# A decoder trunk on one core: a tile's square and copy after its low part, and column sums and spreads at other places among the matmuls

## The chip, the cores and the metric

The kernel runs on one core of a Trainium2 chip. The metric is the device time of the program in microseconds (us). Before the change it is 1248.27 us, the median of three runs (1246.43 to 1250.76). The engines are TensorE (PE: matmuls; its weight loads are listed as PEld), VectorE (DVE), ScalarE (ACT), GpSimd (POOL) and SyncE (SP, which issues DMAs). Each works through its own list of instructions in order and waits at the head of that list when something that it needs isn't ready.

## The reference

Two layers over 512 tokens of 1024 channels, in float32. Layer 0 mixes with a gated short convolution and a forgetting attention, layer 1 with a convolution module; each is followed by a SwiGLU feed-forward part. Around every part stands a normalisation before and one after:

```python
def rms_norm(x, g):
    xf = x.astype(jnp.float32)
    y = xf * lax.rsqrt(jnp.mean(xf * xf, axis=-1, keepdims=True) + RMS_EPS)
    return (y * g.astype(jnp.float32)).astype(x.dtype)

u = rms_norm(h, norm_mix_pre[layer])
h = h + rms_norm(m, norm_mix_post[layer])          # m = mixer(u)
f = swiglu_ffn(rms_norm(h, norm_ffn_pre[layer]), w_ffn_in[layer], w_ffn_out[layer])
h = h + rms_norm(f, norm_ffn_post[layer])
```

Between two parts, then, stand the closing norm of one, the residual sum, and the opening norm of the next. The kernel calls this stretch `cross`; this text calls it a handover.

## The kernel before

Channels lie on the 128 partitions, eight tiles `h[k]` of 128 channels, and the 512 tokens along the free side, in two halves of 256 columns. A matmul keeps float32 precision by splitting both operands into a high and a low part (`wh`, `wl`, `xh`, `xl`) and summing three products: high by high, high by low, low by high (`mm3`, lines 197 to 199). Weights arrive in chunks of 512 KB (`ensure`): an SP DMA fills `wr`, ACT rounds it to `wh` (line 175), and DVE (line 177) or POOL (line 180) takes the rest as `wl`. PE's order is the order in which the code is written.

There are three handovers, called H1 to H3 here: after the mixer of layer 0, after the feed-forward part of layer 0, and after the mixer of layer 1. In them ACT, DVE and POOL keep the written order too (`manual_schedule`, line 842). A handover runs so:

- `tail(0)` and `tail(1)` are the last matmuls of the old part, for the first and the second half of the columns. An output `m` that is finished is squared and copied out by ACT (`evict`).
- The squares are summed over the eight `m` in `acc` (line 240: POOL, the last one DVE). Two matmuls with a column of ones give the column sums (line 257, called column sums below). DVE takes a reciprocal root of them in eleven small Newton steps (lines 299 to 309), and two matmuls with the identity spread the result over all partitions (line 317, called a spread).
- `tiles(hf, n)` then makes the new activations of one half, tile by tile. For tile `k`: DVE multiplies the output by the spread (line 707, into `t`), does the low part of the tile before (`low(k - 1)`, line 702, `xl`), and adds the residual (line 712) into `hp`, which stands in one of two PSUM banks by turns; ACT rounds `hp` to the high part `xh` (line 714), squares it for the next norm (line 713's call, seen as line 247), and copies it to `h[k]` (line 717). After the eighth tile, `xl` comes first and copy and square after it (lines 718 to 721). Newton steps of another norm are put between these DVE instructions by `beside()`.
- `quads` multiplies the first four weight chunks of the next part with one half of the columns: eight steps `k` with eight matmuls each on `xh[k]` (lines 794 and 795), then eight steps of four matmuls on `xl[k]` (line 797). It runs for half 0, then for half 1. `pairs` goes on with both halves.
- `weave(units, inserts)` sets the order: after unit `n` of the matmuls stand the instructions whose number is `n`.

So PE stands still at a column sum until the squares are summed, at a spread until the Newton steps are done, and at a step of `quads` until its `xh[k]` is there. `scale_pre` (line 725) puts the spread of the opening norm into `R`, by which every result of `quads` is multiplied when it is taken out (`ready`, `evict`).

Of the kernel before, what the change touches and what calls it, by code (L numbers as in the profile page):

```python
# [10 lines left out]
AF = mybir.ActivationFunctionType  # L11
# [6 lines left out]
NK = D // P  # L18
# [14 lines left out]
MIXF0 = 0  # L33
MIXF1 = 3
MIXF2 = 0
FIRST_TILE = 14
STATS1 = 1
TILES1 = 5
PRE0 = 8
SCALE0 = 2  # L40
PRE1 = 10
SCALE1 = 4
END0 = 5
END1 = 18
# [44 lines left out]
def trunk(tc, x, vec, bands, w_xa, w_in, w_v, w_f, w_out, w_fi, w_fo, w_p1, w_p2, out):  # L89
# [6 lines left out]
    act = nc.scalar.activation  # L96
# [5 lines left out]
    with tc.tile_pool(name="sb", bufs=1) as sb, tc.tile_pool(  # L102
# [4 lines left out]
        def alloc(tag, shape=(P, T), dt=F32, bufs=1):  # L107
            uid[0] += 1
            return sb.tile(list(shape), dt, name=f"{tag}_{uid[0]}", tag=tag, bufs=bufs)
# [46 lines left out]
        def ensure(n, pieces=1):  # L156

            while len(split) < min(n, len(chunks)):
                name, ap, spare = chunks[len(split)]
                count[name] = count.get(name, -1) + 1  # L160
                raw = alloc("wr", (P, D), F32, 2)
                if spare is None:
                    h = alloc("wh", (P, D), FR, 5)
                    l = alloc("wl", (P, D), FR, 5)
                else:
                    if spare == 0:
                        spares[0] = alloc("pth", (P, 2560), FR), alloc("ptl", (P, 2560), FR)
                    h, l = (t[:, spare * D : (spare + 1) * D] for t in spares[0])
                a = ap.shape[1]
                r3 = raw.rearrange("p (a b) -> p a b", a=a)  # L170
                for i in range(pieces):
                    cs = slice(i * D // pieces, (i + 1) * D // pieces)
                    ps = slice(i * a // pieces, (i + 1) * a // pieces)
                    nc.sync.dma_start(r3[:, ps], ap[:, ps])
                    act(h[:, cs], raw[:, cs], AF.Copy)  # L175
                    if (name, count[name]) not in pool_split:
                        tt(out=l[:, cs], in0=raw[:, cs], in1=h[:, cs], op=ALU.subtract)  # L177
                        continue
                    for c in range(i * D // pieces, (i + 1) * D // pieces, HT):
                        nc.gpsimd.tensor_tensor(out=l[:, c : c + HT], in0=raw[:, c : c + HT], in1=h[:, c : c + HT],  # L180
                                                op=ALU.subtract)
                split.append((name, h, l))
# [28 lines left out]
        def col(i, n=1):  # L211
            return vecs[:, i : i + n]
# [47 lines left out]
        def weave(units, inserts=()):  # L260

            todo = list(inserts)
            n = 0
            while todo and todo[0][0] <= 0:
                todo.pop(0)[1]()
            for _ in units:
                n += 1
                while todo and todo[0][0] <= n:
                    todo.pop(0)[1]()
            for _, f in todo:  # L270
                f()
# [40 lines left out]
        def spread(*cols, tag="s", ps=None):  # L312

            if ps is None:
                ps = psum(tag)
            for j, c in enumerate(cols):
                mm(ps[:, j * P : (j + 1) * P], c.to_broadcast([P, P]), ident, start=True, stop=True)
            return ps

        def each(t, n):  # L320
            return [t[:, j : j + 1] for j in range(n)]
# [324 lines left out]
        class Boundary:  # L646
# [19 lines left out]
            def evict(self, m, ps, c0, cn, part=None):  # L666
                cs = slice(c0, c0 + cn)
                extra = {} if self.bias is None else {"bias": col(self.bias + m)}
                src = ps
                with tc.high_priority():  # L670
                    if part is not None:
                        tt(out=self.s[m][:, cs], in0=ps, in1=part[:, cs], op=ALU.add)
                        src = self.s[m][:, cs]
                        extra = {}
                    for c in range(c0, c0 + cn, HT):
                        self.sums.square(c // HT, src[:, c - c0 : c - c0 + HT], m == NK - 1,
                                         room=self.bank(0)[:, HT:] if m == NK - 1 else None, **extra)
                    if part is None:
                        act(self.s[m][:, cs], ps, AF.Identity if extra else AF.Copy, **extra)  # L679
# [12 lines left out]
            def tiles(self, hf, beside):  # L692

                cs = slice(hf * HT, (hf + 1) * HT)
                if hf == 0:
                    self.pre = Sums()
                rp = spread(*each(self.cols[hf], 2), ps=self.bank(1)[:, :HT])
                t = self.bank(1)[:, HT:]

                def low(k):  # L700
                    hp, g = self.hp
                    stt(out=self.x[1][k][:, cs], in0=hp, scalar=g, in1=self.x[0][k][:, cs],  # L702
                        op0=ALU.mult, op1=ALU.subtract)
                    beside()

                for k in range(NK):
                    stt(out=t, in0=self.s[k][:, cs], scalar=col(self.gpost + k), in1=rp, op0=ALU.mult, op1=ALU.mult)
                    beside()
                    if k:
                        low(k - 1)  # L710
                    hp, g = self.hp = self.bank(2 + k % 2)[:, :HT], col(self.gpre + k)
                    tt(out=hp, in0=hin[k][:, cs], in1=t, op=ALU.add)  # L712
                    beside()
                    act(self.x[0][k][:, cs], hp, AF.Copy, scale=g)  # L714
                    if k < NK - 1:
                        self.pre.square(hf, hp, False)
                        act(hin[k][:, cs], hp, AF.Copy)
                    yield
                low(k)
                act(hin[k][:, cs], hp, AF.Copy)  # L720
                self.pre.square(hf, hp, True, room=self.bank(2 + k % 2)[:, HT:])
                yield
# [92 lines left out]
        def cross(bd, tail, name, evict):  # L815


            held, side = {}, [iter(())]

            def beside():  # L820
                next(side[0], None)

            def begin(gen):
                side[0] = gen

            def rest():
                for _ in side[0]:
                    pass

            def ready(hf):  # L830
                bd.scale_pre(hf)
                for p in range(2):
                    evict(p, held[hf][p][:, 0], held[hf][p][:, 1], bd.R, hf * HT, HT)

            def tiles(hf, n):
                if hf not in gens:
                    gens[hf] = bd.tiles(hf, beside)
                for _ in range(n):
                    next(gens[hf], None)

            gens = {}
            with tc.manual_schedule(engines={mybir.EngineType.Activation, mybir.EngineType.DVE, mybir.EngineType.Pool}):
                weave(tail(0))
                base = cursor[0]
                weave(tail(1), [(1, lambda: ensure(base + 3)), (4, lambda: bd.post0(0)), (10, lambda: ensure(base + 4))]
                      + [(FIRST_TILE + 4 * k, lambda: tiles(0, 1)) for k in range(5)])
                w4 = [take(name, 0) for _ in range(4)]
                weave(quads(w4, bd.x, 0, lambda pb, c0, cn: held.update({0: pb})),
                      [(0, lambda: tiles(0, 1)), (STATS1, lambda: begin(bd.stats_post(1))),
                       (STATS1, lambda: (tiles(0, 3), rest())), (TILES1, lambda: (tiles(1, 2), ensure(base + 5))),  # L850
                       (PRE0, lambda: begin(bd.stats_pre(0))), (PRE0, lambda: (tiles(1, 4), ensure(base + 6)))])
                weave(quads(w4, bd.x, 1, lambda pb, c0, cn: held.update({1: pb})),
                      [(0, lambda: (tiles(1, 3), rest())), (SCALE0, lambda: ready(0)),
                       (PRE1, lambda: (begin(bd.stats_pre(1)), rest()))])
                late = [(SCALE1, lambda: ready(1))]
                weave(pairs(name, bd, 2, 3, evict), late)
# [46 lines left out]
        hin = [alloc(f"h{k}") for k in range(NK)]  # L903
        for k in range(NK):
            nc.gpsimd.dma_start(hin[k], x[:, k])
        bd = Boundary(V_MIX_POST, V_FFN_PRE)
# [8 lines left out]
        bd, tail = ffn(bd, g, V_FFN_POST, V_MIX_PRE + 8)  # L915
# [271 lines left out]
        bd = Boundary(V_MIX_POST + 8, V_FFN_PRE + 8, V_PW2)  # L1187
# [12 lines left out]
        bd, tail = ffn(bd, g, V_FFN_POST + 8, None)  # L1200
# [78 lines left out]
```

## Time and profile before

| | |
|---|---|
| median of the runs | 1248.27 us |
| the profiled execution, its own time | 1246.69 us |
| its span | 1244.9 us |
| granted TensorE clock, mean | 0.978 of full speed |
| busy: PE | 1181.4 us, 95% of the span |
| busy: DVE | 670.0 us, 54% |
| busy: ACT | 515.8 us, 41% |
| busy: POOL | 290.3 us, 23% |

PE is busy nearly all the time, and its work is fixed, so what can be had is its idle time and the time in which its clock is at the lower of its two levels (1.2 instead of 2.4 GHz). In the page's 40 slices of 31 us PE shows an 8 or a 7 where the handovers lie (from 218, 622 and 840 us), and the granted clock an 8 in these slices or the one after. The trace is then read around these places.

### The profile page before, as it was taken

How to read it: one execution, taken by the hardware profiler on the slowest of the kernel's cores; microseconds unless marked ns; L12 is line 12 of the kernel's file. 1: busy time of each engine (PE TensorE's matmuls, PEld its weight loads, DVE VectorE, ACT ScalarE, POOL GpSimd, SP SyncE). 2: the span in 40 equal slices, each digit the busy share in tenths (PEclk: the TensorE clock that was granted, in tenths of full speed). 3: DMA queues.
4: the chain of work that ended last, by engine and by line, in shares of the span. 5: the costliest groups of instructions: out<-in, count | busy, mean ns of one | idle time of the engine just before them, and what ended most of it. 6: DMA issues, size and time to landing. Idle time of an engine off the chain costs nothing.

```text
span 1244.9 us, 16224 instructions
## 1 busy us (share of the span) xinstructions
PE 1181.4 (95%) x6134; PEld 1003.2 (81%) x6134; DVE 670.0 (54%) x1240; ACT 515.8 (41%) x958; POOL 290.3 (23%) x373
## 2 busy tenths in 40 slices
PE   8899999899999999999979999797999999999995
PEld 6677777898888888888978888797888888888884
DVE  6568884465442234443368989826644413444426
ACT  4356773653332223332345674555533322323320
POOL 4243442732000000001534589044300000000010
PEclk9899999989999999999989999898999999999997
DMA  5332222414333333333303443031343332333312
GB/s 176 105 116 85 85 74 96 120 35 123 97 102 93 94 101 87 99 102 90 97 17 114 159 147 100 1 84 36 87 133 88 99 102 85 102 102 90 97 34 68
DMA packets 43118, 115.88 MB, mean 93 GB/s; under 512 B 4696, under 2 KB 14040, under 8 KB 43040
## 3 DMA queue, kind: packets, MB, share of 16 engines
q1 hardware_dynamic: 39936, 109.30, 29.9%
q10 hardware_dynamic: 2384, 3.15, 0.8%
q0 software_dynamic: 720, 2.39, 0.6%
q8 instruction: 48, 0.79, 0.3%
q14 instruction: 30, 0.25, 0.1%
HBM read 109.05 MB, written 5.78 MB: 92 GB/s over the span
## 4 chain that ended last, share of the span: by engine, by line
PE 79%; DVE 9%; ACT 6%; DMA 2%; issue 2%; POOL 1%; SPq 0%; DVEq 0%; ACTq 0%; POOLq 0%
PE pg L199 23%; PE pg L197 23%; PE pg L198 22%; ACT xh L714 2%; DVE xl L702 1%; PE pg L797 1%; PE pg L794 1%; PE pg L795 1%; DVE ps L712 1%; PE pp L560 1%; DVE wl L177 1%; PE po L985 1%; ACT sq L247 1%; PE ps L539 1%; DMA wr<-w_fi 1%
## 5 line engine op out<-in xcount | busy, mean ns | idle before, releaser
L197 PE MATMUL pg<-xh,wh 128*128 128x512 f32 (+1 forms) x960 | 371.2, 387 | 0.0
L198 PE MATMUL pg<-xl,wh 128*128 128x512 f32 (+1 forms) x960 | 367.2, 383 | 3.0 <-DVE xl L350 3.0
L199 PE MATMUL pg<-xh,wl 128*128 128x512 f32 (+1 forms) x960 | 367.8, 383 | 1.2 <-DVE wl L177 1.2
L175 ACT ACTIVATE wh<-wr 128x1024 fp32r<-128x1024 f32 (+1 forms) x186 | 193.1, 1041 | 412.0 <-PE pg L198 332.1
L177 DVE TENSOR_TENSOR wl<-wr,wh 128x1024 fp32r<-128x1024 f32 (+1 forms) x145 | 176.0, 1215 | 176.3 <-ACT wh L175 176.2
L240 POOL TENSOR_TENSOR acc<-acc,sq 128x256 f32<-128x256 f32 x106 | 85.3, 817 | 747.7 <-ACT sq L247 747.1
L198 PEld LDWEIGHTS pg<-xl,wh 128*128 128x128 f32 x960 | 180.7, 188 | 37.7 <-DVE xl L350 3.8
L199 PEld LDWEIGHTS pg<-xh,wl 128*128 128x128 f32 x960 | 180.5, 188 | 37.5 <-DVE wl L177 2.3
L197 PEld LDWEIGHTS pg<-xh,wh 128*128 128x128 f32 x960 | 181.0, 189 | 34.4 <-issue 0.7
L197 PE MATMUL pg<-z,wh 128*128 128x512 f32 (+1 forms) x514 | 182.1, 354 | 0.0
L198 PE MATMUL pg<-z,wh 128*128 128x512 f32 (+1 forms) x514 | 181.0, 352 | 0.8 <-DVE z L410 0.8
L199 PE MATMUL pg<-z,wl 128*128 128x512 f32 (+1 forms) x514 | 181.1, 352 | 0.0
L180 POOL TENSOR_TENSOR wl<-wr,wh 128x256 fp32r<-128x256 f32 x164 | 132.5, 839 | 120.3 <-ACT wh L175 119.9
L198 PEld LDWEIGHTS pg<-z,wh 128*128 128x128 f32 x514 | 96.7, 188 | 15.6 <-DVE z L410 1.2
L197 PEld LDWEIGHTS pg<-z,wh 128*128 128x128 f32 x514 | 96.7, 188 | 14.6 <-ACT m L679 0.3
L199 PEld LDWEIGHTS pg<-z,wl 128*128 128x128 f32 x514 | 96.7, 188 | 14.4
L869 DVE TENSOR_TENSOR t<-pg,R 128x512 f32<-128x512 f32 (+1 forms) x48 | 31.0, 645 | 120.5 <-PE pg L199 120.5
L867 DVE TENSOR_TENSOR t<-pg,R 128x512 f32<-128x512 f32 (+1 forms) x48 | 31.0, 646 | 82.0 <-PE pg L199 79.3
L1007 DVE SCALAR_TENSOR_TENSOR ps<-z,vecs,ps 128x512 f32<-128x512 f32 x69 | 49.0, 748 | 0.6 <-ACT ps L1004 0.2
L794 PE MATMUL pg<-xh,wh 128*128 128x256 f32 x160 | 44.8, 305 | 1.2 <-ACT xh L1180 1.2
L795 PE MATMUL pg<-xh,wl 128*128 128x256 f32 x160 | 44.3, 302 | 0.0
L871 ACT ACTIVATE z<-t 128x512 fp32r<-128x512 f32 (+1 forms) x48 | 28.7, 598 | 34.9 <-DVE t L870 34.9
(257 smaller groups left out, 1444.9 us busy)
## 6 DMA issues: line engine op xcount, KB each, us to landing
wr<-w_fi SPq DMA_DIRECT2D x88, 512.0 KB
wr<-w_fo SPq DMA_DIRECT2D x44, 512.0 KB
wr<-w_p SPq DMA_DIRECT2D x24, 512.0 KB
wr<-w_in SPq DMA_DIRECT2D x16, 512.0 KB
wr<-w_out SPq DMA_DIRECT2D x8, 512.0 KB
h<-x SPq DMA_DIRECT2D x8, 256.0 KB
wr<-w_xa SPq DMA_DIRECT2D x8, 256.0 KB
wr<-w_v SPq DMA_DIRECT2D x4, 512.0 KB
```

The costliest lines, as they stand in the source:

```text
L175: act(h[:, cs], raw[:, cs], AF.Copy)
L177: tt(out=l[:, cs], in0=raw[:, cs], in1=h[:, cs], op=ALU.subtract)
L180: nc.gpsimd.tensor_tensor(out=l[:, c : c + HT], in0=raw[:, c : c + HT], in1=h[:, c : c + HT], op=ALU.subtract)
L197: mm(ps, wh, xh, start=first, stop=False)
L198: mm(ps, wh, xl, start=False, stop=False)
L199: mm(ps, wl, xh, start=False, stop=last)
L240: eng.tensor_tensor(out=acc, in0=acc, in1=t, op=ALU.add)
L794: mm(ps, wh, xt[0][k][:, cs], start=k == 0 and m % 2 == 0, stop=False)
L795: mm(ps, wl, xt[0][k][:, cs], start=False, stop=False)
L867: tt(out=tg, in0=pg, in1=R[:, cs], op=ALU.mult)
L869: tt(out=tu, in0=pu, in1=R[:, cs], op=ALU.mult)
L1007: stt(out=a if j < n - 1 else res, in0=u[:, j : j + T], scalar=w_col(i, j), in1=a, op0=ALU.mult, op1=ALU.add)
```

## The change

In `tiles`, the square of tile `k - 1` and its copy move into the round of tile `k`, behind `xl[k - 1]`; `xh[k]` stands between the two. The places of the inserts move: in `tail(1)` the column sums of half 0 from unit 4 to 6, the first tile from 14 to 13, the others 4.25 apart; in `quads` of half 0 the column sums of half 1 from unit 1 to 3, their spread from 5 to 8, the column sums of the opening norm from 8 to 9; in `quads` of half 1 the spread of `R` from 2 to 5, the taking out of half 0 from 2 to 7, the column sums of half 1 from 10 to 12. Nothing is added or taken away: each engine has as many instructions as before.

```diff
-FIRST_TILE = 14
-STATS1 = 1
-TILES1 = 5
-PRE0 = 8
-SCALE0 = 2
-PRE1 = 10
+STATS0 = 6
+TILES0 = 13
+STATS1 = 3
+TILES1 = 8
+PRE0 = 9
+SCALE0 = 5
+PRE1 = 12
...
                     if k:
                         low(k - 1)
+                        old = self.hp[0]
+                        self.pre.square(hf, old, False)
                     hp, g = self.hp = self.bank(2 + k % 2)[:, :HT], col(self.gpre + k)
                     tt(out=hp, in0=hin[k][:, cs], in1=t, op=ALU.add)
                     beside()
                     act(self.x[0][k][:, cs], hp, AF.Copy, scale=g)
-                    if k < NK - 1:
-                        self.pre.square(hf, hp, False)
-                        act(hin[k][:, cs], hp, AF.Copy)
+                    if k:
+                        act(hin[k - 1][:, cs], old, AF.Copy)
                     yield
...
                 weave(quads(w4, bd.x, 1, lambda pb, c0, cn: held.update({1: pb})),
-                      [(0, lambda: (tiles(1, 3), rest())), (SCALE0, lambda: ready(0)),
+                      [(1, lambda: tiles(1, 1)), (2, lambda: (tiles(1, 1), ensure(base + 6))),
+                       (4, lambda: (tiles(1, 1), rest())), (SCALE0, lambda: bd.scale_pre(0)),
+                       (6, lambda: tiles(1, 3)), (7, lambda: evicts(0)),
                        (PRE1, lambda: (begin(bd.stats_pre(1)), rest()))])
```

ACT in H2, the first tiles of half 1, before (`xh_864` is tile 0, `xh_865` tile 1; `ps_5115` and `ps_5116` are the two banks of `hp`, `acc` and `sq` the squares, `h` the copies):

```order
L714 ACTIVATE xh_864_4707<-ps_5115,vecs_74 128x256
L247 ACTIVATE acc_5205<-ps_5115 128x256
L717 ACTIVATE h_458_2065<-ps_5115 128x256
L714 ACTIVATE xh_865_4708<-ps_5116,vecs_74 128x256
L247 ACTIVATE sq_5400<-ps_5116 128x256
L717 ACTIVATE h_459_2066<-ps_5116 128x256
L175 ACTIVATE wh_5405<-wr_5404 128x1024
```

The same place now (lines are two or three numbers higher):

```order
L717 ACTIVATE xh_864_4707<-ps_5115,vecs_74 128x256
L248 ACTIVATE acc_5216<-ps_5115 128x256
L717 ACTIVATE xh_865_4708<-ps_5116,vecs_74 128x256
L719 ACTIVATE h_458_2065<-ps_5115 128x256
L176 ACTIVATE wh_5435<-wr_5434 128x1024
L248 ACTIVATE sq_5464<-ps_5116 128x256
L717 ACTIVATE xh_866_4709<-ps_5115,vecs_74 128x256
```

The copy of tile 0 (`h_458`) now stands behind `xh` of tile 1, and the square of tile 1 behind the weight conversion.

PE in H2, around the column sums of half 1 (`acc_4771`) in `quads` of half 0, before:

```order
L794 MATMUL pg_5318<-xh_864_4707,wh_5175 128x256
L795 MATMUL pg_5318<-xh_864_4707,wl_5176 128x256
L257 MATMUL pp_5113<-ones_72,acc_4771 128x1 x2
L794 MATMUL pg_5317<-xh_865_4708,pth_5041 128x256
L795 MATMUL pg_5317<-xh_865_4708,ptl_5042 128x256
```

And now:

```order
L796 MATMUL pg_5314<-xh_866_4709,wh_5175 128x256
L797 MATMUL pg_5314<-xh_866_4709,wl_5176 128x256
L258 MATMUL pp_5113<-ones_72,acc_4771 128x1 x2
L796 MATMUL pg_5313<-xh_867_4710,pth_5041 128x256
L797 MATMUL pg_5313<-xh_867_4710,ptl_5042 128x256
```

They stood behind the step of tile 0, and now stand behind that of tile 2: two steps of eight matmuls later.

DVE in H2, tiles 1 and 2 of half 1, where a weight chunk's low part is DVE's own, before:

```order
L712 TENSOR_TENSOR ps_5116<-h_459_2066,po_5114 128x256
L177 TENSOR_TENSOR wl_5406<-wr_5404,wh_5405 128x1024
L707 SCALAR_TENSOR_TENSOR po_5114<-m_681_3557,vecs_74,po_5114 128x256
L299 TENSOR_SCALAR pp_5113<-pp_5113 128x2
L702 SCALAR_TENSOR_TENSOR xl_873_4716<-ps_5116,vecs_74,xh_865_4708 128x256
```

And now:

```order
L715 TENSOR_TENSOR ps_5116<-h_459_2066,po_5114 128x256
L306 TENSOR_TENSOR pp_5113<-pp_5113,st_y_5422 128x2
L178 TENSOR_TENSOR wl_5436<-wr_5434,wh_5435 128x1024
L708 SCALAR_TENSOR_TENSOR po_5114<-m_681_3557,vecs_74,po_5114 128x256
L308 SCALAR_TENSOR_TENSOR pp_5113<-pp_5113,st_y_5422 128x2
L703 SCALAR_TENSOR_TENSOR xl_873_4716<-ps_5116,vecs_74,xh_865_4708 128x256
```

The weight's low part stays between tile 1 and tile 2; the Newton steps of the opening norm begin one tile earlier, so the second and fourth of them now stand around it.

## Rows read from the trace of the kernel before

**Rows 1.** Waits of PE, whole span: waiting line, releaser, us in total, times, longest.

```profile
PE pp L257 <- DVE acc L240: 20.4, 7, 6.4
```

**Rows 2.** Timeline of PE in H1: start, us, engine, line, operation, [idle before <-releaser].

```profile
257.05 0.71 PE L317 MATMUL po<-eye,st_y 128*128 128x128 f32 x4 [0.66 <-DVE st_y L309]
...
268.30 0.71 PE L317 MATMUL pp<-eye,st_y 128*128 128x128 f32 x4 [1.54 <-DVE st_y L309]
...
278.54 0.40 PE L797 MATMUL pg<-xl,wh 128*128 128x256 f32 x2
...
281.80 0.71 PE L317 MATMUL pp<-eye,st_y 128*128 128x128 f32 x4
```

**Rows 3.** Timeline of PE in H2.

```profile
626.40 0.61 PE L257 MATMUL pp<-ones,acc 128*128 128x1 f32 x4 [2.35 <-DVE acc L240]
...
634.38 0.71 PE L317 MATMUL po<-eye,st_y 128*128 128x128 f32 x4 [1.95 <-DVE st_y L309]
...
648.15 1.22 PE L317 MATMUL pp<-eye,st_y 128*128 128x128 f32 x4 [4.05 <-DVE st_y L309]
...
659.82 0.40 PE L797 MATMUL pg<-xl,wh 128*128 128x256 f32 x2
```

**Rows 4.** Timeline of PE in H3.

```profile
853.94 1.02 PE L257 MATMUL pp<-ones,acc 128*128 128x1 f32 x4 [6.40 <-DVE acc L240]
...
861.93 0.71 PE L317 MATMUL po<-eye,st_y 128*128 128x128 f32 x4 [0.98 <-DVE st_y L309]
...
883.41 0.40 PE L797 MATMUL pg<-xl,wh 128*128 128x256 f32 x2
```

**Rows 5.** Timeline of DVE in H2, tiles and last square.

```profile
616.41 0.43 DVE L712 TENSOR_TENSOR ps<-h,po 128x256 f32<-128x256 f32 x1
...
617.93 0.48 DVE L702 SCALAR_TENSOR_TENSOR xl<-ps,vecs,xh 128x256 fp32r<-128x256 f32 x1 [0.57 <-ACT h L717]
...
618.33 0.42 DVE L712 TENSOR_TENSOR ps<-h,po 128x256 f32<-128x256 f32 x1
...
625.92 0.42 DVE L240 TENSOR_TENSOR acc<-acc,pp 128x256 f32<-128x256 f32 x1 [1.43 <-ACT pp L247]
...
627.05 0.42 DVE L712 TENSOR_TENSOR ps<-h,po 128x256 f32<-128x256 f32 x1
...
630.93 0.15 DVE L309 SCALAR_TENSOR_TENSOR st_y<-pp,st_y 128x2 f32<-128x2 f32 x1
...
631.00 0.42 DVE L712 TENSOR_TENSOR ps<-h,po 128x256 f32<-128x256 f32 x1
...
631.96 0.48 DVE L702 SCALAR_TENSOR_TENSOR xl<-ps,vecs,xh 128x256 fp32r<-128x256 f32 x1 [0.47 <-ACT xh L714]
...
635.65 0.43 DVE L712 TENSOR_TENSOR ps<-h,po 128x256 f32<-128x256 f32 x1
...
640.03 1.23 DVE L177 TENSOR_TENSOR wl<-wr,wh 128x1024 fp32r<-128x1024 f32 x1 [2.04 <-ACT wh L175]
```

**Rows 6.** Timeline of ACT: two rows of H1, two of H2, one of H3.

```profile
239.56 0.46 ACT L714 ACTIVATE xh<-ps,vecs 128x256 fp32r<-128x256 f32 x1
...
272.43 0.48 ACT L714 ACTIVATE xh<-ps,vecs 128x256 fp32r<-128x256 f32 x1 [0.89 <-DVE ps L712]
...
616.88 0.48 ACT L714 ACTIVATE xh<-ps,vecs 128x256 fp32r<-128x256 f32 x1 [1.24 <-DVE ps L712]
...
625.42 0.40 ACT L247 ACTIVATE pp<-pg 128x256 f32<-128x256 f32 x1
...
844.12 0.48 ACT L714 ACTIVATE xh<-ps,vecs 128x256 fp32r<-128x256 f32 x1 [2.05 <-PE pg L199]
```

**Rows 7.** PE in stretches of H2: length, busy (matmuls), granted clock, DMA share, GB/s.

```profile
628.00:630.00 2.00, 2.00 (x12) 0.50 0.00 0
...
632.00:634.00 2.00, 0.43 (x4) 1.00 0.00 0
```

**Rows 8.** The page's groups: busy us, mean ns of one, idle before and its releaser.

```profile
L175 ACT ACTIVATE wh<-wr 128x1024 fp32r<-128x1024 f32 (+1 forms) x186 | 193.1, 1041 | 412.0 <-PE pg L198 332.1
```

More of the change, by code (lines that the diff above doesn't have):

```diff
@@ L831, in ready, with evicts @@
                 bd.scale_pre(hf)
+                evicts(hf)
+            def evicts(hf):
                 for p in range(2):
@@ L844, in cross @@
                 base = cursor[0]
-                weave(tail(1), [(1, lambda: ensure(base + 3)), (4, lambda: bd.post0(0)), (10, lambda: ensure(base + 4))]
-                      + [(FIRST_TILE + 4 * k, lambda: tiles(0, 1)) for k in range(5)])
+                weave(tail(1), [(1, lambda: ensure(base + 3)), (STATS0, lambda: bd.post0(0)), (10, lambda: ensure(base + 4))]
+                      + [(TILES0 + 17 * k // 4, lambda: tiles(0, 1)) for k in range(5)])
                 w4 = [take(name, 0) for _ in range(4)]
@@ L849, in cross @@
                       [(0, lambda: tiles(0, 1)), (STATS1, lambda: begin(bd.stats_post(1))),
-                       (STATS1, lambda: (tiles(0, 3), rest())), (TILES1, lambda: (tiles(1, 2), ensure(base + 5))),
-                       (PRE0, lambda: begin(bd.stats_pre(0))), (PRE0, lambda: (tiles(1, 4), ensure(base + 6)))])
+                       (STATS1, lambda: (tiles(0, 3), rest())), (TILES1, lambda: tiles(1, 1)),
+                       (PRE0, lambda: begin(bd.stats_pre(0))), (PRE0, lambda: (tiles(1, 1), ensure(base + 5))),
+                       (14, lambda: tiles(1, 1))])
                 weave(quads(w4, bd.x, 1, lambda pb, c0, cn: held.update({1: pb})),
-                      [(0, lambda: (tiles(1, 3), rest())), (SCALE0, lambda: ready(0)),
+                      [(1, lambda: tiles(1, 1)), (2, lambda: (tiles(1, 1), ensure(base + 6))),
+                       (4, lambda: (tiles(1, 1), rest())), (SCALE0, lambda: bd.scale_pre(0)),
+                       (6, lambda: tiles(1, 3)), (7, lambda: evicts(0)),
                        (PRE1, lambda: (begin(bd.stats_pre(1)), rest()))])
```

## Prediction

> **What bounds the kernel now.** The table of busy times comes first: PE is busy for 95% of the span, so the end moves only if PE waits less or runs less at its lower clock. PE's waits come next [rows 1]: the column sums at line 257 alone cost it 20.4 us in seven waits. Its timeline then shows where: each handover has a wait at the column sums of half 1, one at their spread and one at the spread of `R`. In H2 these are 2.35, 1.95 and 4.05 us [rows 3], in H3 the first two are 6.40 and 0.98 [rows 4], in H1 the last two 0.66 and 1.54 [rows 2]. All wait for DVE, and DVE is no more than half busy: so it is a chain that is late, not an engine that is full.
>
> The timeline of DVE shows the chain [rows 5]. One tile takes 1.92 us (line 712 at 616.41 and again at 618.33). `xl` at 617.93 sat idle for 0.57 and was released by ACT's `h`, the copy, though what it computes needs only `xh`. So a tile is: residual sum, `xh` 0.47 later (616.41 to 616.88, rows 6), square, copy, then `xl`, then the next residual sum 0.40 later. The eighth tile shows the other order: its `xl` stands ahead of square and copy and starts 0.96 after its sum (631.00 to 631.96), released by `xh` itself.
>
> **The change, part by part.** *The new order in the tile.* All tiles now run as the eighth did: 0.96 from sum to `xl` and 0.40 from `xl` to the next sum [rows 5], 1.36 instead of 1.92 us. Where a Newton step stands between the two it adds 0.07 (630.93 to 631.00): 1.43. The square and copy are hidden under DVE's next tile: the square can start when `xl` ends, 0.48 after it began, and the next `xh` comes 0.40 + 0.47 after that begin, so about 0.4 is free for a square that holds ACT no longer than its 0.40 [rows 6]. Were that cover gone, each tile would get longer by up to that 0.40. The lower end of the pace is thus 1.36, the upper 1.92 (the copy still waited for in some way); I take 1.36 since the row of the eighth tile is the very order that all have now.
>
> *From the spread of half 0 to that of half 1.* Five tiles run beside `tail(1)`, and the sixth waits behind DVE's sum of the last square (line 240). What follows that sum is fixed: 1.13 to the sixth tile's residual sum (625.92 to 627.05), two tiles, and 3.38 from the eighth's to the spread (631.00 to 634.38, rows 3 and 5). The last square itself stands on ACT behind the fifth tile's `xh` and one copy, 0.48 and some 0.4, and DVE's sum comes 0.50 after it begins.
> - H1: the first `xh` starts at 239.56 [rows 6]. Four tiles at 1.36 give 245.0, the square starts at 245.9, its sum 246.4, sixth tile 247.5, eighth 250.4, spread 253.8 instead of 257.05: 3.3 gained.
> - H3: the first `xh` had to wait for PE (844.12, rows 6), since it is written over a tile that PE still reads. The same chain gives 858.3 instead of 861.93: 3.6 gained. PE may come to that point earlier, since its column sums of half 0 stand later too; I leave that out.
> - H2: here the tiles are done early and `tail(1)` sets the last square. PE ran dry at 624.05 (626.40 less 2.35), one step of `quads` after the tail. A step of eight matmuls is 0.95: from 268.30 to 278.94 in H1 [rows 2], 10.6 us hold six such steps, eight of half the length, a spread, sums and the last matmul's end. So the square can start at 623.1, the sixth tile's sum stands at 624.7, the eighth's at 627.6, the spread at 631.0. PE itself gets there at 624.05 + 7 x 0.95 + 0.4 = 631.1. But DVE's first Newton step now waits for column sums that stand two steps later, which can hold its queue, with `xl` behind it, for up to 0.7. I take 631.5 instead of 634.38: 2.9 gained.
>
> Together 9.8 us. The waits at the column sums (6.40 in H3) need not be taken off as well: they lie inside these stretches.
>
> *From the spread of half 1 to the end of `quads`.* Before, PE took 21.9 us in H1 and H3 (257.05 to 278.94, 861.93 to 883.81) and 25.8 in H2 (634.38 to 660.22). What is late next is the last `xh` of half 1: PE's step on it and eight half steps follow. From the spread: 1.27 to the first residual sum (634.38 to 635.65), seven tiles, four at 1.43 and three at 1.36, 9.8; 0.47 to `xh` and 0.48 for it; 0.95 for its step, 3.8 for the half steps, 0.7 for sums and the end. Two weight conversions of 1.04 [rows 8] stand in ACT's list between these tiles; a tile leaves ACT some 0.4 free, so each costs between 0 and 1.0, and I take 0.5 twice. The sum is 18.5, so 3.4 gained in H1 and in H3. In H2 DVE also does the low part of a weight: before it sat 2.04 for `wh` and worked 1.23 [rows 5]; now `wh` stands behind tile 1's `xh` and a copy, so this costs much the same, 2.4 beyond the 0.5 already counted. 20.9, so 4.9 gained there, in which the wait of 4.05 goes and its slow stretch behind it.
>
> Together 11.7 us. The spread of `R` is no term: its Newton steps are through before PE's fifth step, as the same eleven steps take four tiles.
>
> *Given back.* The spread of `R` for half 1 stands four steps into `pairs`. In H1 it came 9.4 us after the last `xh` (272.43 to 281.80) and PE had no wait there, though the chain (sum of squares, taking out of half 0, an activation table's load, Newton) was only just through. PE now comes there some 8.7 after that `xh` began (0.48, 0.95, 3.8, 0.7 and 2.8 us for twelve matmuls of 512 columns, each twice the 0.12 of 256, an eighth of the step). I count 0.8 in H1, 0.3 in H3, nothing in H2. Taking out half 0 moves from unit 2 to 7 on paper only: on DVE and ACT it stood behind the last tile before, and does now. DMAs keep their order on SP; POOL's list has the same work, its weight parts a tile or two earlier. I price that at 0 (bounds 0 and the 0.5 of one square's sum three times).
>
> Sum: 9.8 + 11.7 - 1.1 = 20.4 us. The profiled execution took 1246.69, so 1226.3. The median of the runs shown is 1.6 above that execution: 1228.
>
> **The clock.** After 2.35 us of idleness in H2 the granted clock was 0.50 from 628 to 630, its lower level of 1.2 GHz; with PE busy for 0.43 of the 2 us from 632 it stayed at 1.00 [rows 7]. The new order turns a few long waits into many short ones: a step of 0.95 per tile of 1.36 to 1.43 leaves PE idle for 0.4 to 0.5 us eight times over. By the second row that costs nothing, and the sum takes that. The Trainium skill (TensorE: Matmul & The Clock Gate, "A second HAM failure mode: psum-queue depth-cycling") tells of a kernel whose short, frequent idle moments between groups of matmuls sent the clock up and down. By that rule part of the gain would be lost; no stretch of this trace has such a pattern with these matmuls for long, so the trace leaves it open. It is the third rival below.
>
> **The rivals.**
> - *Half the pace.* ACT and DVE now wait for each other twice in a tile (`xl` for `xh`, the square for `xl`). If the square holds up `xh`, or POOL's sums hold up the squares' three buffers, a tile takes the middle of 1.36 and 1.92. About half of the 21.5 goes: 1248.3 - 10 = 1238. For it: ACT's margin of 0 to 0.4 a tile. Against it: ACT's work of a tile, a copy, a square and an `xh`, is below 1.36.
> - *The chain doesn't move.* `xl` still waits for the copy, or something behind it takes its place; the later places of column sums and spreads then only move waits. 1247 to 1248. Against it: the eighth tile's row, and that each instruction that `xl` had to pass is gone from ahead of it.
> - *The lower clock through half 1.* The price: eight steps of 1.9 instead of tiles of 1.4, 4.0 us; eight half steps 3.8 more; the first twelve matmuls of `pairs` 2.8. That is 10.6 in each handover, 32 in all, against 20.4 gained: 1260. It decides from about two thirds of that stretch on, in all three. Against it are the rows of 632 to 634; a single slow stretch costs 2 to 3 us and stays inside my range.
>
> **How the numbers follow.** The forecast, 1221 to 1236, has 0.70; half the pace, 1236 to 1244, 0.18; no move 0.07; the slower clock 0.05. What this kernel's measurement can tell from no change is about 0.3%, 3.7 us: all of the first two is below 1244.5. So faster 0.88, same 0.07, slower 0.05. The low end is every wait of the three handovers gone: 17.9 us in the seven named above, some 5 in H1's first and H3's last, which I take for like their neighbours, and 4 to 5 for slow stretches behind them, 28 in all: 1220. The high end takes in most of the half pace: 1240.
>
> **What would show it.** Right: line 703 (`xl`) released by `xh` with about 0.5 of idleness less; residual sums 1.4 apart in half 1; PE's waits at the column sums of half 1 below 1 us in H1 and H2 and below 2.5 in H3; spreads of half 1 with waits of 1 to 2; small new waits of PE for `xh` in `quads` of half 1; 18 to 19 us from spread to end in H1 and H3. Wrong: sums 1.6 or more apart, the square of a tile with idleness before it that ends at `xl` while the next `xh` stands ready, or a granted clock of 0.50 in half 1 of `quads`.

## The result, and the profile after

The changed kernel takes 1227.71 us (median of 4 runs, 1224.52 to 1230.15) against 1247.38 for the kernel before beside it (4 runs): a ratio of 0.9829, 95% interval 0.9812 to 0.9847. The forecast was 1228, in a range of 1220 to 1240. The profiled execution after took 1230.15, with a span of 1228.4; PE is busy for 96% of it.

PE's waits after, in the columns of [rows 1]:

```profile
PE pp L258 <- DVE acc L241: 8.5, 5, 3.9
...
PE pg L796 <- ACT xh L717: 2.0, 6, 1.1
PE pp L318 <- DVE st_y L310: 1.7, 2, 0.9
```

And before, the row of the spreads of `R`, which [rows 1] doesn't show:

```profile
PE pp L317 <- DVE st_y L309: 7.1, 3, 4.1
```

The column sums cost 8.5 us instead of 20.4, and the spreads of `R` cost 1.7 in two waits instead of 7.1 in three. New is the middle row after, the waits for `xh` in `quads`. Line numbers are one or more higher than before. The timeline of PE shows where, first H1 (to be held beside [rows 2]), then H2 ([rows 3]) and H3 ([rows 4]):

```profile
246.83 0.60 PE L258 MATMUL pp<-ones,acc 128*128 128x1 f32 x4 [0.65 <-DVE acc L241]
...
253.72 0.71 PE L318 MATMUL po<-eye,st_y 128*128 128x128 f32 x4 [1.19 <-DVE st_y L310]
...
266.73 0.38 PE L796 MATMUL pg<-xh,pth 128*128 128x256 f32 x1
...
271.79 0.40 PE L799 MATMUL pg<-xl,wh 128*128 128x256 f32 x2
...
275.80 0.71 PE L318 MATMUL pp<-eye,st_y 128*128 128x128 f32 x4 [0.86 <-DVE st_y L310]
...
625.67 0.71 PE L318 MATMUL po<-eye,st_y 128*128 128x128 f32 x4 [0.55 <-DVE st_y L310]
...
633.61 0.38 PE L796 MATMUL pg<-xh,pth 128*128 128x256 f32 x1 [1.08 <-ACT xh L717]
...
637.52 0.60 PE L318 MATMUL pp<-eye,st_y 128*128 128x128 f32 x4
...
646.12 0.40 PE L799 MATMUL pg<-xl,wh 128*128 128x256 f32 x2
...
840.81 0.61 PE L258 MATMUL pp<-ones,acc 128*128 128x1 f32 x4 [2.26 <-DVE acc L241]
847.70 0.71 PE L318 MATMUL po<-eye,st_y 128*128 128x128 f32 x4
...
865.76 0.40 PE L799 MATMUL pg<-xl,wh 128*128 128x256 f32 x2
...
869.75 0.71 PE L318 MATMUL pp<-eye,st_y 128*128 128x128 f32 x4 [0.84 <-DVE st_y L310]
```

The reader is to see three things. The spread of half 1 in H1 starts at 253.72 instead of 257.05, and the end of `quads` (the row of line 799, where line 797 stood before) at 271.79 instead of 278.54. The wait of 4.05 in H2 is gone (637.52 has none). And the spread of `R` for half 1, which had no wait before, now has one of 0.86 in H1 and 0.84 in H3.

DVE's timeline in H1 shows the tiles, as [rows 5] did in H2:

```profile
256.44 0.42 DVE L715 TENSOR_TENSOR ps<-h,po 128x256 f32<-128x256 f32 x1
...
257.40 0.48 DVE L703 SCALAR_TENSOR_TENSOR xl<-ps,vecs,xh 128x256 fp32r<-128x256 f32 x1
...
257.87 0.42 DVE L715 TENSOR_TENSOR ps<-h,po 128x256 f32<-128x256 f32 x1
...
259.26 0.48 DVE L703 SCALAR_TENSOR_TENSOR xl<-ps,vecs,xh 128x256 fp32r<-128x256 f32 x1 [0.38 <-ACT xh L717]
...
259.73 0.42 DVE L715 TENSOR_TENSOR ps<-h,po 128x256 f32<-128x256 f32 x1
...
266.71 0.48 DVE L703 SCALAR_TENSOR_TENSOR xl<-ps,vecs,xh 128x256 fp32r<-128x256 f32 x1 [0.54 <-ACT xh L717]
```

From 256.44 to 257.87 a tile takes 1.43 us; `xl` has no idleness, or is released by `xh`, and no longer by the copy. The next tile takes 1.86 (257.87 to 259.73): a weight conversion stands before its `xh` on ACT.

### The profile page after: what moved, and what is told of

The parts are those of the page before. It is cut to its first block, busy times and chain, and to the rows that moved or that the text cites. A ratio compares the mean times of both kernels' runs of the same rounds, so it can differ in the third digit from the quotient of the medians.

```text
span 1228.4 us, 16273 instructions
## 1 busy us (share of the span) xinstructions
PE 1178.8 (96%) x6134; PEld 997.8 (81%) x6134; DVE 669.9 (55%) x1240; ACT 516.4 (42%) x958; POOL 289.6 (24%) x373
## 3 DMA queue, kind: packets, MB, share of 16 engines
q0 software_dynamic: 720, 2.39, 0.6%
## 4 chain that ended last, share of the span: by engine, by line
PE 75%; DVE 11%; DMA 4%; ACT 4%; POOL 3%; issue 3%; SPq 0%; DVEq 0%; ACTq 0%; POOLq 0%
PE pg L198 22%; PE pg L199 22%; PE pg L200 22%; DVE ps L1015 2%; PE pg L796 1%; PE pg L797 1%; DVE wl L178 1%; PE pp L561 1%; ACT wh L176 1%; DMA wr<-w_p 1%; POOL wl L181 1%; DMA wr<-w_fi 1%; POOL acc L241 1%; PE ps L540 1%; PE po L580 1%
```

## The experiments

Theory 1 is that of the prediction: the chain square, sum, Newton steps, spread, tiles sets the end of a handover, so the tile's pace is what the change bought; the places only let PE work while the chain runs. Theory 2, the rival: PE waited because sums and spreads stood too early among its matmuls, and the order within a tile matters little. e1 to e4, e5 to e8 and e9 to e11 were each measured together, on one chip and beside the same runs of the kernel before.

| kernel | us | ratio to before (95%) |
|---|---|---|
| changed | 1227.71 | 0.9829 (0.9812 to 0.9847) |
| e1 order alone | 1230.48 | 0.9859 (0.9841 to 0.9876) |
| e2 places alone | 1244.59 | 0.9970 (0.9960 to 0.9980) |
| e3 square first | 1235.53 | 0.9895 (0.9879 to 0.9910) |
| e4 later spread of `R` | 1230.31 | 0.9852 (0.9833 to 0.9871) |
| e5 H2's `wl` on POOL | 1226.23 | 0.9830 (0.9814 to 0.9847) |
| e6 later sums and spread | 1230.05 | 0.9861 (0.9847 to 0.9874) |
| e7 weights behind the tiles | 1229.91 | 0.9858 (0.9845 to 0.9872) |
| e8 a later `wl` on POOL | 1227.47 | 0.9839 (0.9825 to 0.9853) |
| e9 changed, again | 1229.13 | 0.9850 (0.9834 to 0.9866) |
| e10 both `wl` on POOL | 1225.30 | 0.9819 (0.9805 to 0.9834) |
| e11 e10, `R` one step later | 1224.57 | 0.9816 (0.9802 to 0.9830) |

**e1, the order alone.** The kernel before with this part of the change only:

```diff
                     if k:
                         low(k - 1)
+                        old = self.hp[0]
+                        self.pre.square(hf, old, False)
...
-                    if k < NK - 1:
-                        self.pre.square(hf, hp, False)
-                        act(hin[k][:, cs], hp, AF.Copy)
+                    if k:
+                        act(hin[k - 1][:, cs], old, AF.Copy)
```

> The kernel before with the new order in a tile alone (xl ahead of square and copy); column sums and spreads at their old places. Theory 1 (the chain through the tiles sets the end, and the places only let PE work while it runs): the stretch from the spread of half 0 to that of half 1 gains its 9 to 10 us. Behind the spread nothing is gained, since it still stands one step into quads: PE then has 7 x 0.95 + 8 x 0.48 of half 0 and 8 x 0.95 + 8 x 0.48 of half 1 ahead of it, 22 us, as long as the 21.9 of before. So about 1237, and residual sums 1.4 apart. Theory 2 (PE waited because its column sums and spreads stood too early; the order in a tile matters little): 1244 to 1248.

Measured: 1.41% off, 17.6 us, where some 11 (1237) were expected; theory 2 falls. From the spread of half 0 to that of half 1 the three handovers gain 3.5, 3.3 and 2.8, together 9.6 as expected. The miss lies behind the spread, where 7.0 more are gained and nothing was expected (20.1, 22.5 and 20.0 us to the end of `quads`, before 21.9, 25.8 and 21.9). It is an error of reading: the column sums of half 1 stand one step into `quads`, but their spread stands five steps in (`TILES1`). So PE had three steps of 0.95 of half 0 behind the spread, and not the seven that I counted. The windows of PE from the spread to the end of `quads` in H1, of the changed kernel (first fence) and of e1 (columns: busy, granted clock, DMA share, GB/s):

```profile
253.72:272.19 18.47, 18.05 (x145) 1.00 0.20 58
```

```profile
254.54:274.64 20.10, 20.10 (x169) 1.00 0.19 53
```

In e1 PE is busy all the time, 20.10 us: there PE's own list sets the end. In the changed kernel, with 24 matmuls fewer behind the spread, it is busy for 18.05 of 18.47. This is what the places are for: in the profiles they take 4.8 us more off the stretches behind the spreads, and give 1.7 back at the spread of `R`. In time this step isn't shown, as the intervals of e1 and the changed kernel lie over each other.

**e2, the places alone.** The changed kernel with the lines of e1 turned back.

> The changed kernel with the old order in a tile (square and copy ahead of xl). Theory 1: the chain keeps its pace of 1.9 us a tile, so the waits at the column sums of half 1 get shorter, but PE waits for xh in half 1 of quads and at the spread instead: 1243 to 1250, close to before. Theory 2: most of the gain, 1227 to 1233.

Measured: 0.30% off, 3.7 us, as theory 1 had it. DVE's timeline in H1 and PE's waits:

```profile
261.27 0.42 DVE L713 TENSOR_TENSOR ps<-h,po 128x256 f32<-128x256 f32 x1
...
262.78 0.48 DVE L703 SCALAR_TENSOR_TENSOR xl<-ps,vecs,xh 128x256 fp32r<-128x256 f32 x1 [0.50 <-ACT h L718]
...
263.25 0.42 DVE L713 TENSOR_TENSOR ps<-h,po 128x256 f32<-128x256 f32 x1
```

```profile
PE pg L795 <- ACT xh L715: 10.2, 16, 1.9
```

The copy (`h`, line 718) still releases `xl`, tiles are 1.98 apart, and PE's waits turn up as 16 waits for `xh`, 10.2 us. The two parts, 1.41% and 0.30%, come to 1.71%; the whole change took 1.71% in the first measurement and 1.50% in e9, so the intervals allow that they add up, and don't show it.

**e3, the square ahead of `xl`, the copy behind.**

```diff
                     act(self.x[0][k][:, cs], hp, AF.Copy, scale=g)
+                    if k < NK - 1:
+                        self.pre.square(hf, hp, False)
                     if k:
                         act(hin[k - 1][:, cs], old, AF.Copy)
```

(and the square behind `low` taken out)

> The changed kernel with the square of a tile ahead of its xl again, and the copy behind it. If each reader of the tile on ACT that stands ahead of xl costs its own time (1.92 less 1.36, 0.56 for the two), residual sums stand 1.64 apart and about half of the 20 us is lost: 1236 to 1240. If only the copy was in the way (the releaser that the trace named): 1.36 to 1.43 apart and 1226 to 1230. If any reader ahead of xl costs the whole wait: 1.9 apart and 1243 to 1250.

```profile
259.81 0.42 DVE L714 TENSOR_TENSOR ps<-h,po 128x256 f32<-128x256 f32 x1
...
261.04 0.49 DVE L703 SCALAR_TENSOR_TENSOR xl<-ps,vecs,xh 128x256 fp32r<-128x256 f32 x1 [0.22 <-ACT sq L248]
...
261.51 0.42 DVE L714 TENSOR_TENSOR ps<-h,po 128x256 f32<-128x256 f32 x1
```

Now it is the square that releases `xl`, and with a Newton step between a tile takes 1.70: 1.64 and 0.07, the first of the three cases. The time lies just under its 1236. So it was not the copy as such: each reader of the tile on ACT that stands ahead of `xl` costs 0.27 to 0.28 us a tile (1.70 less 1.43, 1.98 less 1.70). The Trainium skill (PSUM — Partial Sum Buffer, "PSUM bank collisions raise a hardware error") says that the compiler's scheduler adds a dependency between any two instructions on different engines that touch the same bank and the same 32 partitions, "reads and writes alike". The rows agree in that square, copy and `xl` all only read the tile, and `xl` still waited 0.22 for the square in e3 and 0.50 for the copy in e2; what put the order there they don't show.

**e4, the spread of `R` for half 1 two steps later.** `SCALE1 = 6` instead of 4.

> The changed kernel with the spread of R for half 1 two steps later in pairs (after six instead of four). Theory 1: the waits of 0.86 in H1 and 0.84 in H3 go, since 1.4 us of matmuls stand between now; nothing else moves: 1.5 to 1.7 us less than the changed kernel, 1226. Rival: what R releases (taking out of half 1) comes later by the same 1.4 us and PE waits for a bank in the next chunk of pairs instead: no difference.

No difference that can be told. The waits of 0.86 and 0.84 are gone. But behind H2 PE waits longer for a weight's low part (0.46 in the changed kernel), and its clock falls after it:

```profile
663.73 0.50 PE L200 MATMUL pg<-xh,wl 128*128 128x512 f32 x1 [1.80 <-DVE wl L178]
```

```profile
664.00:666.00 2.00, 2.00 (x8) 0.72 0.61 133
666.00:668.00 2.00, 2.00 (x6) 0.50 0.91 297
```

The rival was right in kind: what `R` holds up is not a bank but DVE's list. The low part of that weight stands behind the taking out of half 1 in it, and begins 17.4 us after the end of `quads` in H2 (662.06 after 644.64) instead of 16.1 (662.58 after 646.52).

**e5, H2's `wl` on POOL.** Entry 4 of `SPLIT1` is `P` instead of `D`.

> The changed kernel with the low part of H2's weight chunk on POOL instead of DVE. In its H2, DVE sat 1.70 for wh and worked 1.23 on wl between two tiles. If the tiles of half 1 set the end there, the stretch from spread to the end of quads falls from 20.9 toward 18.5, as in the other two, and DVE, busy for most of the convolution stage, gets its 1.2 back there too: 1.5 to 3 us less than the changed kernel, 1225 to 1226. Rival: POOL, which adds the squares, is later by four pieces of 0.7, and the column sums behind it take the gain: within 1 of 1227.7.

```profile
626.57 0.71 PE L318 MATMUL po<-eye,st_y 128*128 128x128 f32 x4 [0.55 <-DVE st_y L310]
...
644.62 0.40 PE L799 MATMUL pg<-xl,wh 128*128 128x256 f32 x2
```

From spread to the end of `quads` H2 now takes 18.45 (644.62 + 0.40 - 626.57) instead of 20.85 (646.12 + 0.40 - 625.67), the 2.4 that were expected. The median is 1.5 lower than the changed kernel's, but the ratio to the kernel before is the same (0.9830 and 0.9829): in the time of one kernel against the other that isn't shown.

**e6, column sums and spread of half 1 still later.** `STATS1 = 5`, `TILES1 = 9`, `PRE0 = 10`.

> The changed kernel with the column sums of half 1 two steps of quads later and their spread one step later (STATS1 5, TILES1 9, PRE0 10). PE's waits of 0.65, 1.19 and 2.26 at these places lose what PE now does ahead of them. Theory 1 (the chain sum, Newton steps, spread, tiles of half 1 sets the end; in the changed kernel PE waits for the last xh by 0.05 to 0.15): the waits go, PE waits for xh instead, and the time stays within 1.5 of 1227.7. Rival (PE's own list behind the spread sets the end, since it was busy for 18.05 of 18.47 us from spread to end in H1): 3 to 4 us less, 1224.

```profile
249.20 0.50 PE L258 MATMUL pp<-ones,acc 128*128 128x1 f32 x4
...
255.09 0.71 PE L318 MATMUL po<-eye,st_y 128*128 128x128 f32 x4 [0.72 <-DVE st_y L310]
```

```profile
PE pg L796 <- ACT xh L717: 5.3, 14, 1.6
```

The waits at the column sums of half 1 are gone, and waits for `xh` rise from 2.0 to 5.3 us: nothing won. The median, 1230.05, lies outside the 1.5 that theory 1 allowed, but whether something is lost can't be told, as its interval lies over those of the changed kernel and of e9. In the trace H2 lost: there the column sums of half 1 had no wait in the changed kernel, and two steps later they only start the Newton steps later; from the column sums of half 0 to the end of `quads` H2 takes 42.5 us instead of 40.6; H1 takes 39.3 instead of 39.1, and H3 41.0 instead of 40.9. In the changed kernel, then, PE's own list is not what sets the end, the chain is.

**e7, both weight conversions behind the last tile.**

```diff
-(PRE0, lambda: (tiles(1, 1), ensure(base + 5))),
+(PRE0, lambda: tiles(1, 1)),
...
-(2, lambda: (tiles(1, 1), ensure(base + 6))),
+(2, lambda: tiles(1, 1)),
...
-(6, lambda: tiles(1, 3)), (7, lambda: evicts(0)),
+(6, lambda: (tiles(1, 3), ensure(base + 6))), (7, lambda: evicts(0)),
```

> The changed kernel with both weight conversions of half 1 behind its last tile on ACT, and so out of the chain of tiles. Theory 1: the chain loses 0.5 twice in H1 and H3 and some 3.4 in H2 (the wait of 1.70 and DVE's 1.23, and 0.5), as far as PE's own list behind the spread, about 17.5 us, lets it: 1 us in H1 and in H3 and 3 in H2, 1222 to 1224. Rival: the conversions end too late for pairs (two of 1.04 on ACT and a low part on POOL of 2.8 behind them, some 5 us after the last xh, and PE comes there 5.5 after it): waits for wl, 1227 to 1231.

```profile
254.44:272.55 18.11, 17.82 (x145) 1.00 0.01 1
```

```profile
277.90 1.01 PE L318 MATMUL pp<-eye,st_y 128*128 128x128 f32 x3 [2.60 <-DVE st_y L310]
```

The gain up to the end of `quads` is there: 18.1 us from the spread in each handover (in the changed kernel 18.47, 20.85 and 18.46), PE busy for 17.82 in H1. That is 3.5 us. But the time is no better, which was the rival's number; its reason was another. The conversions, 1.99 us on ACT, now stand ahead of the taking out of half 0 and of the sums behind it, and the spread of `R` waits 2.60 instead of 0.86 (0.96 instead of nothing in H2, 1.21 instead of 0.84 in H3): 3.1 us are given back.

**e8, another `wl` on POOL.** Entry 10 of `SPLIT1`. The convolution stage between H2 and H3 had looked 3 us longer after the change than before, and DVE sat 2.77 us there.

> The changed kernel with the low part of one weight chunk in the convolution stage behind H2 on POOL instead of DVE. That stage took 3 us longer in the changed kernel's profile than before; there DVE was busy for 9.5 to 10 of 10 us in most stretches and sat 2.77 for wh ahead of this low part (0.49 before). If DVE is what bounds the stage, up to 1.9 + 2.8 us come back: 1224 to 1226. If DMAs or POOL (busy 8 to 10 of 10 in places) set it: within 1 of 1227.7, or later.

**e9, the changed kernel again.**

> The changed kernel itself, once more, beside the two below. If the 3 us by which its convolution stage was longer in the first profile belong to the change, the stretch from the end of quads in H2 to that in H3 is again near 219.6 us and its column sums wait some 127 to 128 us behind the end of quads; if they come and go with the landing of DMAs, the stretch is anywhere from 217 to 220 (217.0 and 217.2 were seen in two of the kernels that differ little). Median 1226 to 1229 in either case.

e8's time is that of the changed kernel (its second case), and e9 shows that its question was wrong. From the end of `quads` in H2 to that in H3 the first profile of the changed kernel took 219.64 us (646.12 to 865.76), the second 214.56 (646.39 to 860.95). That is less than either case of its expectation had. The program is the same, and up to 646 the two agree within 0.3. PE's timeline in the second profile:

```profile
646.39 0.40 PE L799 MATMUL pg<-xl,wh 128*128 128x256 f32 x2
...
860.95 0.40 PE L799 MATMUL pg<-xl,wh 128*128 128x256 f32 x2
```

DVE's low part of a weight, again the second profile and then the first:

```profile
672.15 1.23 DVE L178 TENSOR_TENSOR wl<-wr,wh 128x1024 fp32r<-128x1024 f32 x1 [1.19 <-ACT wh L176]
```

```profile
673.47 1.87 DVE L178 TENSOR_TENSOR wl<-wr,wh 128x1024 fp32r<-128x1024 f32 x1 [2.77 <-ACT wh L176]
```

ACT's `wh` ahead of this `wl` waited 0.68 for its DMA in the one and 2.34 in the other:

```profile
671.06 1.06 ACT L176 ACTIVATE wh<-wr 128x1024 fp32r<-128x1024 f32 x1 [0.68 <-DMA wr<-w_p]
```

```profile
672.38 1.06 ACT L176 ACTIVATE wh<-wr 128x1024 fp32r<-128x1024 f32 x1 [2.34 <-DMA wr<-w_p]
```

So the 3 us can't be laid to the change: the stage varies by 5 us with no change at all. The wait for this weight (2.34 and 0.68) is the first large difference between the two profiles there. Why that DMA landed later was not tried, nor whether all of the 5 us come from it. The stage's 5.1 us cover the 4.8 between the two profiled executions (1230.15 and 1225.34). That it also spreads the other seven times of the changed kernel (all nine reach from 1224.5 to 1230.7) is likely, but no trace shows it.

**e10 and e11, both `wl` on POOL, and with it `SCALE1 = 5`.**

> The changed kernel with two low parts on POOL instead of DVE: H2's and that of the convolution stage. If the 2.4 us that the first took from the way to the end of quads in H2, and what the second took off the convolution stage, add up: 2 to 4 us below the changed kernel of this same call. If the convolution stage takes back what H2 gains: within 1.5 of it.

> The same with the spread of R for half 1 one step later in pairs. Its waits of 0.86 in H1 and 0.84 in H3 get 0.7 of matmuls ahead of them: up to 1.4 us below e10. Rival: as with the spread two steps later, what R releases comes later and a weight's low part behind it too, so no difference, or 1 to 2 us more where PE waits for that weight.

e10 is 3.8 and e11 4.6 us below e9, which was measured beside them; the intervals of e10 and e9 touch at 0.9834, that of e11 ends at 0.9830. In e11 the wait for `R` in H1 is down to 0.20:

```profile
276.82 0.71 PE L318 MATMUL pp<-eye,st_y 128*128 128x128 f32 x4 [0.20 <-DVE st_y L310]
```

All eight times of the two lie between 1224.05 and 1226.56. So they beat the kernel before by 1.8%. Against the changed kernel beside them the step is about 0.3%, and only e11's interval is clear of it, narrowly; against the changed kernel's first measurement (0.9829) it is not shown. e11 against e10 can't be told apart. The profiles show H2's part of it: from the end of `quads` in H1 to that in H2 e10 takes 371.96 us and e9 374.35. What the low part in the convolution stage gave they don't show, for that stage took 218.14 us in e10, between the 214.56 and 219.64 of the changed kernel.

## Why the prediction was right

| term | foretold | measured |
|---|---|---|
| tile of half 1 with, without Newton step | 1.43, 1.36 | 1.43 to 1.44, 1.36 to 1.37 |
| weight conversion between tiles | 0.5 | 0.43 and 0.49 |
| to the spread of half 1: H1, H2, H3 | 3.3, 2.9, 3.6 | 3.3, 2.8, 3.3 |
| spread to the end of `quads`: H1, H2, H3 | 18.5, 20.9, 18.5 | 18.47, 20.85, 18.46 |
| wait for `R` of half 1: H1, H2, H3 | 0.8, 0, 0.3 | 0.86, 0, 0.84 |

How the third row is worked out: H1 by the same place in both traces (257.05 less 253.72); H3 from the first `xh`, which PE releases (844.12 to 861.93 before [rows 4, 6], 833.23 to 847.70 after: 17.81 less 14.47); H2 from the ends of `quads` in H1 and H2, 381.28 apart before (278.54 to 659.82) and 374.33 after (271.79 to 646.12), a gain of 6.95, of which 4.99 came behind the spread and 0.86 was lost at `R`. Together the last three rows gain 9.4 and 11.8 and lose 1.7: 19.5 us instead of the 20.4 that were forecast. That the median came within 0.3 us of the 1228 is luck: the spans of the two profiles of the changed kernel lie 16.5 and 21.3 us below that of the kernel before.

*The pace* was the right reason, and the row of the eighth tile the right one to take it from; e3 shows that it holds reader by reader. e1 shows that the order brings most of the gain. The rival *half the pace* would have had ACT hold `xh`; the residual sums of half 1, 1.36 to 1.44 apart where no weight conversion stands between, say that it doesn't.

*What is late behind the spread* was only half right. I named the last `xh` of half 1. It does end last (in H1 PE starts on it at 266.73, when `xl` does too, 266.71), but by less than half a microsecond: PE is busy for 18.05 of the 18.47. I hadn't added up PE's own list. For e1 I did add it up, but from the wrong place. The waits of 1 to 2 us at the spreads of half 1, which I had named as a sign, came in H1 only (1.19; 0.55 in H2, none in H3).

*The clock.* From 628 to 640 in H2, with a wait of 1.08 and four of about 0.2 in it, the granted clock stayed at 1.00 (windows of the changed kernel, PE):

```profile
628.00:640.00 12.00, 10.12 (x77) 1.00 0.16 44
...
842.00:844.00 2.00, 2.00 (x13) 0.55 0.00 0
844.00:846.00 2.00, 2.00 (x13) 0.60 0.00 0
...
852.00:866.00 14.00, 13.60 (x110) 1.00 0.25 76
```

So the third rival did not come. But the pattern that it needed hardly came either: PE was to stand idle for 0.4 to 0.5 us eight times in each handover. Behind the spread of half 1 it did so three times in H1 and in H3, for 0.09 to 0.15, and six times in H2, once for 1.08 and else for 0.15 to 0.22. It is e2, with its longer tiles, that comes near the pattern. In its H1 PE waits five times between 264 and 274, for 0.24 to 0.76 us, and the clock stays at 1.00:

```profile
264.00:274.00 10.00, 7.25 (x53) 1.00 0.24 60
```

The rule that stood beside the rival (the Trainium skill, TensorE: Matmul & The Clock Gate, "A second HAM failure mode: psum-queue depth-cycling") tells of short, frequent idle moments that send the clock up and down; in this stretch of e2 they did not. What still costs some is a long wait: in H3, after the 2.26 at the column sums, the clock is 0.55 to 0.60 for four microseconds, in half 0 of `quads`, in a stretch where the chain hides it. That there would be no slow stretch in half 1 held for all three handovers (the last row above is H3's).

*Given back* was counted at 1.1 and is 1.7, H3's 0.84 where 0.3 stood. Not foreseen was how far the convolution stage varies from one execution to the next: between the two profiles of the changed kernel it moved the total by 5 us, a quarter of the gain.

## What to carry to other kernels

When a row's releaser only reads what the waiting instruction reads, look for another place for that reader: put the instruction that others wait for first, and let what has slack stand in the shadow of the next tile; the price of each reader ahead can be read from one tile that happens to have the other order. Places of waiting instructions on the bound engine are worth a second look only after the chain is short: add up both the chain and that engine's own list behind the same row, since the longer one answers. And before a stage that the change doesn't touch is explained, profile the same program twice.

## What the runs showed of the hardware that was not expected

The length of PE's idleness alone doesn't say whether its clock falls. After a wait of 1.80 us (e4, above) it was 0.50, after one of 2.26 it was 0.55, and after the 2.60 of e7 it was 0.50 from 278 to 280 us. In H1 of e1, PE waited 2.38 us at the spread of half 1 and the clock stayed at 1.00; in H2 of the same execution it waited 2.39 at the same place, and the clock fell to 0.50:

```profile
254.54 0.71 PE L317 MATMUL po<-eye,st_y 128*128 128x128 f32 x4 [2.38 <-DVE st_y L309]
```

```profile
254.00:256.00 2.00, 1.46 (x12) 1.00 0.00 0
256.00:258.00 2.00, 2.00 (x20) 1.00 0.00 0
```

```profile
626.39 1.22 PE L317 MATMUL po<-eye,st_y 128*128 128x128 f32 x4 [2.39 <-DVE st_y L309]
```

```profile
626.00:628.00 2.00, 1.61 (x7) 0.50 0.04 8
```

And one and the same instruction of one program took 1.23 us in one execution and 1.87 in the other (DVE's `wl` in e9 and in the first profile, above). What differs beside it is POOL: in the first profile a multiplication on POOL had begun at 672.20, ahead of this `wl` (673.47), and in e9 it began at 672.43, behind it (672.15). The first profile of the changed kernel has 137 such low parts of a weight on DVE. In seven of them, those that took 1.31 to 1.87 us, POOL was at work when they began; the other 130, where POOL stood idle or began later, took 1.21 to 1.23. That POOL is the cause was not tested.
